# Hybrid trunk on one core: weight sums take the raw weights' place in the seven-product pairs, early parts get a room, 19 such pairs instead of 17

## The chip, the cores and the metric

The kernel runs on one core of one Trainium2 chip. The metric is the device time of one execution in microseconds (us); the median of three runs is the kernel's time.

## The reference

Two layers act on 256 tokens of 1024 channels: an attention layer and a convolution layer, each followed by an expert mixer ("peer"). What matters here is the mixer's last step. Every token has a gate for some of 16384 experts; the kernel computes all experts densely, so the last line below is, for each layer, one product of a gated activation matrix (256 tokens x 16384 experts) with `expert_v` (16384 x 1024).

```python
def chunk(args):
    xc, ec, gc = args
    u = expert_u[ec]
    act = jax.nn.gelu(jnp.einsum('cd,chkd->chk', xc, u))
    w = gc.astype(xc.dtype) * act
    return jnp.einsum('chk,chkd->cd', w, expert_v[ec])
```

## The kernel before

Each layer's mixer has a first stage, which makes the gated activations (`st`, kept in SBUF with experts on the partitions), and a second stage, which multiplies them with `expert_v` and is called the V stage here. The V stage runs over 64 pairs of weight rows; one row is 128 experts x 1024 channels, 512 KB, and is one load (`raw`, 4 buffers in rotation, issued in order by SP's queue).

Products are float32 in three terms. A float32 operand is split into a high part, rounded to the format that TensorE reads (`hi` for weights, `xh` for activations, cast by ACT), and the remainder (`lo`, `xo`, subtracted by DVE). `mm3` issues hi x hi, hi x lo and lo x hi: three TensorE products of 128x128 by 128x512.

- An **ordinary pair** (`s2`, through `weights`) has 2 rows x 4 quarters of the output (2 token halves by 2 channel halves) x 3 terms = 24 products. For it ACT casts two rows and one activation tile of 512, and DVE makes two `lo` and one `xo`.
- A **seven-product pair** (`s2_seven`; its pair numbers stand in `FAST`) multiplies the two rows as a 2 x 2 block product in Strassen's manner: seven products instead of eight, 21 with the three terms. Before them DVE forms sums of activations (s1 to s4, in place in `st`, 128 columns each) and of weights (t1 to t4, 512 columns each, in a tile of their own, `mix`), and the operands 11, (21, 22), (t1, t3) and (t2, t4) are split: four `hi`/`lo` pairs, all from the rotating room `whl` with three buffers of each. Four of the seven products go to PSUM tiles `q` that collect over all such pairs; `seven_end` adds them into the residual `x` after the last.

The activation parts `xh`/`xo` of ordinary pairs lie in two halves that alternate with the pair's number; a seven-product pair has a third part of its own. So ACT's cast for a pair must wait until TensorE's last product that reads the same part.

Which engine does what, and in which order, is written out at build time: each engine has one instruction stream, whose order a scheduler in the framework fixes; on the chip each stream is followed in order, with semaphore waits for operands and for buffers. In the second half of the first layer's V stage ACT also makes diagonal matrices for the next convolution (`diagonal`), three to a pair.

Of the kernel before, what the change touches and what calls it, by code (L numbers as in the profile page):

```python
# [7 lines left out]
F32 = mybir.dt.float32  # L8
F32R = mybir.dt.float32r
# [6 lines left out]
P = 128  # L16
D = 1024
# [25 lines left out]
G1 = 60  # L43
OH = 3 * NK * TB

FAST = (3, 6, 10, 13, 17, 20, 24, 27, 30, 34, 38, 41, 45, 48, 52, 55, 59)
TMP = 512 + NT * D


# [9 lines left out]
class Trunk:  # L59
# [32 lines left out]
        return cut  # L92


    def load(self, src):
        raw = self.wraw.tile([P, D], F32, tag="raw", name=self.nm("raw"))
        self.last_load = self.nc.sync.dma_start(raw, src)
        return raw

# [88 lines left out]
    def s2_seven(self, acc, q, srcs, a, at, parts, first, last):  # L188

        nc = self.nc
        sub = lambda o, x, y: nc.vector.tensor_tensor(o, x, y, op=ALU.subtract)  # L197
        s1, s2, s4, a11, a21, a12, a22 = (a[:, at + k * P:at + (k + 1) * P] for k in range(-3, 4))
        nc.vector.tensor_tensor(s1, a21, a22, op=ALU.add)
        sub(s2, s1, a11)  # L200
        sub(s4, a12, s2)
        sub(a21, a11, a21)
        ah, ao = parts
        seven = a[:, at - 3 * P:at + 4 * P]
        nc.scalar.copy(ah, seven)
        sub(ao, seven, ah.bitcast(F32))
        A = {k: (ah[:, n * P:(n + 1) * P], ao[:, n * P:(n + 1) * P])
             for n, k in enumerate(("s1", "s2", "s4", "11", "s3", "12", "22"))}
        left, right = slice(0, 512), slice(512, D)
        t1, t3, t2, t4 = (self.mix[:, k, :] for k in range(4))  # L210
        r1, r2 = (self.load(s) for s in srcs)
        sub(t1, r1[:, right], r1[:, left])
        sub(t3, r2[:, right], r1[:, right])
        sub(t2, r2[:, right], t1)
        sub(t4, r2[:, left], t2)
        B = {}
        for v, names in ((r1[:, left], ("11",)), (r2, ("21", "22")),
                         (self.mix[:, 0:2, :].rearrange("p k n -> p (k n)"), ("t1", "t3")),
                         (self.mix[:, 2:4, :].rearrange("p k n -> p (k n)"), ("t2", "t4"))):
            n = 512 * len(names)  # L220
            hi, lo = (self.whl.tile([P, D], F32R, tag=k, name=self.nm(k))[:, 0:n] for k in ("hi", "lo"))
            nc.scalar.copy(hi, v)  # L222
            sub(lo, v, hi.bitcast(F32))
            for k, name in enumerate(names):
                ks = slice(512 * k, 512 * k + 512)
                B[name] = hi[:, ks], lo[:, ks]
        for to, x, y in ((q[1], "11", "11"), (acc[0][0], "12", "21"), (acc[0][1], "s4", "22"),
                         (q[5], "s1", "t1"), (q[7], "s3", "t3"), (q[6], "s2", "t2"), (acc[1][0], "22", "t4")):
            mine = any(to is v for v in q.values())
            self.mm3(to, A[x], B[y], first and mine, last and mine)  # L230

    def seven_end(self, q):

        nc = self.nc
        x = lambda t, h: self.x[:, t, h * 512:(h + 1) * 512]
        one, u = self.mix[:, 0, :], self.mix[:, 1, :]
        add = lambda o, v, w: nc.vector.tensor_tensor(o, v, w, op=ALU.add)
        nc.scalar.copy(one, q[1])
        add(u, q[6], one)
        add(x(0, 0), x(0, 0), one)  # L240
        add(x(0, 1), x(0, 1), u)
        add(x(0, 1), q[5], x(0, 1))
        add(u, q[7], u)
        add(x(1, 0), x(1, 0), u)
        add(x(1, 1), x(1, 1), u)
        add(x(1, 1), q[5], x(1, 1))
# [383 lines left out]
    def peer(self, l, acc):  # L630
        nc, I = self.nc, self.I
        new = lambda: self.store_tile("st").rearrange("p (i t) -> p i t", t=T)
        st = [new()]
        sl = lambda i: st[i // HI][:, i % HI:i % HI + 2, :]

        g = self.gain(2 * l + 1, st[0][:, HI - D // T:, :].rearrange("p i t -> p (i t)"))
        xT = self.norm_T(g, acc)
        U, V = I["u"][l], I["v"][l]
        self.route_open(l)
        for h in range(PH):  # L640
            ps = self.s1_pair([I["wpq"][l, 2 * h], I["wpq"][l, 2 * h + 1]], xT, POOL_Q, h == 0)
            qT = self.qT[h % 2]
            nc.scalar.copy(qT, ps)
            self.route_scores(l, h, qT)
        route = self.route_steps()
        steps = 2 * (PH + 13)
        nb = T // TB
        half = NK // 4
        done = 0
        for pi in range(NK // 2):  # L650
            if pi == G0:
                for _ in route:
                    pass
                st.append(new())
                self.gates_open()
                self.one_hots(0)
            due = min(max(0, pi + 1 - G0) * nb // (G1 - G0), nb)
            todo = list(range(done, due))
            done = due
            ps = self.s1_pair([U[2 * pi], U[2 * pi + 1]], xT,  # L660
                              between=lambda j: [self.gate_bank(b, j, 2 * pi, st) for b in todo])
            for b in todo:
                if b + 1 < nb:
                    self.one_hots(b + 1)
            self.expert_rows(ps, sl(2 * pi), done * TB)
            if pi < G0:
                for _ in range((pi + 1) * steps // G0 - pi * steps // G0):
                    next(route, None)
        acc = self.s2_open()

        wh, wo = (self.one.tile([P, KC * T], F32R, tag=k, name=self.nm(k)) for k in ("xh", "xo"))
        w0 = self.work.tile([P, 2, 2 * T], F32R, tag="oh", name=self.nm("w0"))
        for pi in range(NK // 2):
            flat = st[2 * pi // HI].rearrange("p i t -> p (i t)")
            at = 2 * pi % HI * T
            if pi in FAST:
                fast = slice(4 * T, 4 * T + 7 * P)
                if pi == FAST[0]:
                    self.mix = self.work.tile([P, 4, 512], F32, tag="oh", name=self.nm("mix"))
                    quarters = {k: pool.tile([P, 512], F32, tag=tag, name=self.nm("q"))  # L680
                                for k, pool, tag in ((1, self.ps_m, "ps_m"), (5, self.ps_m, "ps_m"),
                                                     (7, self.ps_h, "ps_h"), (6, self.ps_h, "ps_h"))}
                self.s2_seven(acc, quarters, (V[2 * pi], V[2 * pi + 1]), flat, at, (wh[:, fast], wo[:, fast]),
                              pi == FAST[0], pi == FAST[-1])
            else:
                n = 2 * T
                r = pi % 2 * n

                h, o = (wh[:, r:r + n], wo[:, r:r + n]) if pi else (w0[:, 0], w0[:, 1])
                nc.scalar.copy(h, flat[:, at:at + n])  # L690
                nc.vector.tensor_tensor(o, flat[:, at:at + n], h.bitcast(F32), op=ALU.subtract)  # L691
                parts = [(h[:, j * T:(j + 1) * T], o[:, j * T:(j + 1) * T]) for j in range(2)]
                self.s2(acc, V, parts, 2 * pi, NK)
            if pi == FAST[-1] + 1:
                self.seven_end(quarters)
            if pi < half:
                pass
            elif l + 1 == DEPTH:
                if pi == half:
                    self.g_out = self.gain(2 * DEPTH, self.store_tile("g")[:, 0:D])  # L700
            else:
                if pi == half:
                    prep = self.conv_prep(l + 1)
                for _ in range(-(-(CDG + 1) // half)):
                    next(prep, None)
        return acc
# [280 lines left out]
```

## Time and profile before

| what | value |
|---|---|
| median of three runs | 1868.29 us (1867.66 to 1871.61) |
| profiled execution, its own time | 1868.77 us |
| span of that execution in the profile | 1866.8 us |
| mean granted TensorE clock | 0.996 |
| PE (TensorE products) busy | 1836.3 us, 98% |
| DVE (VectorE) busy | 1484.6 us, 80% |
| ACT (ScalarE) busy | 1006.1 us, 54% |

The span runs from the first to the last instruction; about 2 us of the execution's time lie outside it. PE's busy time counts products that overlap in the pipeline, so the distance between the starts of products, not their length, tells how fast TensorE goes. PEld is its weight load, which runs ahead of the product; an idle time before a PEld row is where TensorE's own queue waits.

### The profile page before, as it was taken

The numbers are of one execution on the slowest core, as the hardware profiler recorded it, in microseconds if no ns is written. First come the engines' busy times: TensorE is split into PE (matmuls) and PEld (weight loads), VectorE is DVE, ScalarE is ACT, GpSimd is POOL, SyncE is SP. The second block draws the span as 40 slices with busy tenths as digits, with TensorE's granted clock in tenths as the row PEclk, the third lists the DMA queues.
The fourth block names the chain that finished last, engine by engine and source line by source line (L and its number), as shares of the span: only waits on it lengthen the run. The fifth ranks groups of instructions, "written<-read, shape, count | busy, mean of one in ns | idle before, by whom it ended". The sixth has DMA issues, their size and how long they took to land. (4 is left out here: it accounts for less than half of the span.)

```text
span 1866.8 us, 32407 instructions
## 1 busy us (share of the span) xinstructions
PE 1836.3 (98%) x12566; PEld 1667.5 (89%) x12566; DVE 1484.6 (80%) x2857; ACT 1006.1 (54%) x1499; POOL 146.2 (8%) x107
## 2 busy tenths in 40 slices
PE   8999999999999999999999899999999999999998
PEld 6879999999999878877798799999999998888786
DVE  4669984788896888888887599847888968888887
ACT  4753455554445565777563534555544455655564
POOL 1213000000000000000076430000000000000000
PEclk9999999999999999999999999999999999999999
DMA  7445555444445656655542355554444456565654
GB/s 271 137 140 177 180 182 182 160 158 159 162 154 181 199 186 208 210 191 194 192 147 68 121 184 173 190 181 159 159 159 159 159 170 210 190 207 197 201 194 142
DMA packets 91738, 326.33 MB, mean 175 GB/s; under 512 B 10176, under 2 KB 12480, under 8 KB 91584
## 3 DMA queue, kind: packets, MB, share of 16 engines
q1 hardware_dynamic: 91584, 324.26, 51.6%
q8 instruction: 98, 1.61, 0.4%
q14 instruction: 56, 0.46, 0.1%
HBM read 323.17 MB, written 1.05 MB: 174 GB/s over the span
## 5 line engine op out<-in xcount | busy, mean ns | idle before, releaser
L108 ACT CAST hi<-raw 128x1024 fp32r<-128x1024 f32 x532 | 557.0, 1049 | 540.6 <-PE ps_h L148 409.3
L148 PE MATMUL ps_h<-xh,hi 128*128 128x256 f32 x2560 | 734.9, 288 | 0.0
L114 DVE TENSOR_TENSOR lo<-raw,hi 128x1024 fp32r<-128x1024 f32 x486 | 592.5, 1221 | 172.3 <-ACT hi L108 170.5
L148 PE MATMUL ps_h<-xh,lo 128*128 128x256 f32 x2560 | 721.5, 283 | 0.0
L148 PE MATMUL ps_h<-xo,hi 128*128 128x256 f32 x2560 | 718.1, 283 | 0.0
L148 PEld LDWEIGHTS ps_h<-xh,hi 128*128 128x128 f32 x2560 | 490.4, 192 | 2.0 <-issue 1.0
L148 PEld LDWEIGHTS ps_h<-xh,lo 128*128 128x128 f32 x2560 | 490.0, 192 | 0.0
L148 PEld LDWEIGHTS ps_h<-xo,hi 128*128 128x128 f32 x2560 | 488.0, 192 | 0.2
L133 PE MATMUL acc<-lo,xh 128*128 128x512 f32 x870 | 338.8, 391 | 1.2 <-DVE lo L197 1.1
L134 PE MATMUL acc<-hi,xo 128*128 128x512 f32 x870 | 337.9, 390 | 0.0
L132 PE MATMUL acc<-hi,xh 128*128 128x512 f32 x870 | 248.8, 391 | 0.0
L133 PEld LDWEIGHTS acc<-lo,xh 128*128 128x128 f32 x870 | 163.5, 188 | 38.2 <-DVE lo L197 2.7
L132 PEld LDWEIGHTS acc<-hi,xh 128*128 128x128 f32 x870 | 163.5, 188 | 34.3 <-ACT hi L108 0.5
L134 PEld LDWEIGHTS acc<-hi,xo 128*128 128x128 f32 x870 | 163.7, 188 | 33.8
L114 POOL TENSOR_TENSOR lo<-raw,hi 128x1024 fp32r<-128x1024 f32 x46 | 109.5, 2387 | 136.3 <-ACT hi L108 117.3
L690 ACT CAST xh<-st 128x512 fp32r<-128x512 f32 x92 | 57.2, 623 | 115.0 <-PE acc L133 115.0
L290 POOL TENSOR_TENSOR sums<-sums,mhalf 128x1 f32<-128x1 f32 x10 | 8.7, 871 | 989.9 <-DVE sums L287 989.9
L691 DVE TENSOR_TENSOR xo<-st,xh 128x512 fp32r<-128x512 f32 x92 | 63.1, 688 | 27.6 <-ACT xh L690 27.5
L197 DVE TENSOR_TENSOR lo<-mix,hi 128x1024 fp32r<-128x1024 f32 x68 | 80.2, 1221 | 5.4 <-ACT hi L222 5.4
L857 DVE TENSOR_TENSOR oh<-iota,slot 128x1024 f16<-128x1024 f16 x64 | 44.3, 692 | 47.8 <-PE ps_g L869 47.8
L869 PE MATMUL ps_g<-oh 128*128 128x128 f16 x1024 | 81.5, 220 | 0.0
L877 DVE SCALAR_TENSOR_TENSOR st<-ps_g,st 128x256 f32<-128x256 f32 (+4 forms) x224 | 74.5, 351 | 8.5 <-PE ps_g L869 8.4
(183 smaller groups left out, 1857.5 us busy)
## 6 DMA issues: line engine op xcount, KB each, us to landing
raw<-in_u_dram SPq DMA_DIRECT2D x256, 512.0 KB, 3.2
raw<-in_v_dram SPq DMA_DIRECT2D x256, 512.0 KB, 4.2
raw<-in_wpq_dram SPq DMA_DIRECT2D x32, 512.0 KB, 3.5
raw<-in_pw_dram SPq DMA_DIRECT2D x24, 512.0 KB, 3.4
raw<-in_wqk_dram SPq DMA_DIRECT2D x16, 512.0 KB, 3.5
raw<-in_wv_dram SPq DMA_DIRECT2D x8, 512.0 KB, 6.6
raw<-in_wo_dram SPq DMA_DIRECT2D x8, 512.0 KB, 3.2
att<-in_bias_dram SPq DMA_DIRECT2D x4, 512.0 KB, 9.1
```

The lines of the kernel that those rows point to most:

```text
L108: ins = [nc.scalar.copy(hi, raw)]
L114: ins.append(eng.tensor_tensor(lo, raw, hi.bitcast(F32), op=ALU.subtract))
L132: return [mm(ps, wh, xh, start=first, stop=False), mm(ps, wh, xo, start=False, stop=False), mm(ps, wo, xh, start=False, stop=last)]
L133: mm(ps, wh, xo, start=False, stop=False),
L134: mm(ps, wo, xh, start=False, stop=last)]
L148: self.nc.tensor.matmul(ps[:, j, :], w[:, c * P:(c + 1) * P], x[:, c, :], start=n == 0, stop=n == len(terms) - 1)
L197: sub = lambda o, x, y: nc.vector.tensor_tensor(o, x, y, op=ALU.subtract)
L690: nc.scalar.copy(h, flat[:, at:at + n])
L691: nc.vector.tensor_tensor(o, flat[:, at:at + n], h.bitcast(F32), op=ALU.subtract)
L857: nc.vector.tensor_tensor(g0, iota, slot(0), op=ALU.is_equal)
L869: nc.tensor.matmul(ps[:, t, :], self.oh[:, b % 2, 0, tp, :, e], self.oh[:, b % 2, 1 + k, tp, :, e], start=k == 0, stop=k == 1)
L877: nc.vector.scalar_tensor_tensor(v, ps[:, :, lo:lo + m].rearrange("p t i -> p i t"), 1.0 / GS, v, op0=ALU.mult, op1=ALU.mult)
```

## The change

`FAST` becomes every third pair, 3 to 57, 19 in each layer instead of 17. In `s2_seven` the sums t1 and t3 overwrite the first raw row and t2 and t4 the second, so `mix` goes; `split` casts and subtracts as before. The parts of the first three weight operands (11, t1 and t3) lie in a tile of their own, `early_room`, which takes the place that `mix` had in SBUF; only (21, 22) and (t4, t2) still take buffers of `whl`. The products stand in another order: the three of `early_room` first. `seven_end` takes its scratch from the `raw` buffers.

```diff
-FAST = (3, 6, 10, 13, 17, 20, 24, 27, 30, 34, 38, 41, 45, 48, 52, 55, 59)
+FAST = tuple(range(3, 60, 3))
...
-        t1, t3, t2, t4 = (self.mix[:, k, :] for k in range(4))
         r1, r2 = (self.load(s) for s in srcs)
-        sub(t1, r1[:, right], r1[:, left])
-        sub(t3, r2[:, right], r1[:, right])
-        sub(t2, r2[:, right], t1)
-        sub(t4, r2[:, left], t2)
-        B = {}
-        for v, names in ((r1[:, left], ("11",)), (r2, ("21", "22")),
-                         (self.mix[:, 0:2, :].rearrange("p k n -> p (k n)"), ("t1", "t3")),
-                         (self.mix[:, 2:4, :].rearrange("p k n -> p (k n)"), ("t2", "t4"))):
-            n = 512 * len(names)
-            hi, lo = (self.whl.tile([P, D], F32R, tag=k, name=self.nm(k))[:, 0:n] for k in ("hi", "lo"))
+
+        def split(v, room, *names):
+            hi, lo = room
             nc.scalar.copy(hi, v)
             sub(lo, v, hi.bitcast(F32))
             for k, name in enumerate(names):
                 ks = slice(512 * k, 512 * k + 512)
                 B[name] = hi[:, ks], lo[:, ks]
-        for to, x, y in ((q[1], "11", "11"), (acc[0][0], "12", "21"), (acc[0][1], "s4", "22"),
-                         (q[5], "s1", "t1"), (q[7], "s3", "t3"), (q[6], "s2", "t2"), (acc[1][0], "22", "t4")):
+        B = {}
+        slot = lambda: [self.whl.tile([P, D], F32R, tag=k, name=self.nm(k)) for k in ("hi", "lo")]
+        split(r1[:, left], self.early_room[0], "11")
+        sub(r1[:, left], r1[:, right], r1[:, left])
+        sub(r1[:, right], r2[:, right], r1[:, right])
+        split(r1, self.early_room[1], "t1", "t3")
+        split(r2, slot(), "21", "22")
+        sub(r2[:, right], r2[:, right], r1[:, left])
+        sub(r2[:, left], r2[:, left], r2[:, right])
+        split(r2, slot(), "t4", "t2")
+        for to, x, y in ((q[1], "11", "11"), (q[5], "s1", "t1"), (q[7], "s3", "t3"), (acc[0][0], "12", "21"),
+                         (acc[0][1], "s4", "22"), (q[6], "s2", "t2"), (acc[1][0], "22", "t4")):
...
-        one, u = self.mix[:, 0, :], self.mix[:, 1, :]
+        room = self.load_room()
+        one, u = room[:, 0:512], room[:, 512:D]
...
-                    self.mix = self.work.tile([P, 4, 512], F32, tag="oh", name=self.nm("mix"))
+                    cut = self.cutter(self.work.tile([P, 6 * 512], F32R, tag="oh", name=self.nm("early")))
+                    self.early_room = [(cut(n), cut(n)) for n in (512, D)]
```

DVE's stream at pair 45 of the second layer, before. The names raw_18732 and raw_18734 are the pair's own two rows; raw_18690 and raw_18696 are the rows of the ordinary pair ahead of it.

```order
L691 TENSOR_TENSOR xo_16851<-st_13397,xh_16850 128x512
L197 TENSOR_TENSOR mix_16967<-raw_18732 128x512
L199 TENSOR_TENSOR st_13397<-st_13397 128x128
L114 TENSOR_TENSOR lo_18693<-raw_18690,hi_18692 128x1024
L197 TENSOR_TENSOR st_13397<-st_13397 128x128 x2
L197 TENSOR_TENSOR mix_16967<-raw_18734,raw_18732 128x512
L197 TENSOR_TENSOR mix_16967<-raw_18734,mix_16967 128x512
L197 TENSOR_TENSOR st_13397<-st_13397 128x128
L114 TENSOR_TENSOR lo_18699<-raw_18696,hi_18698 128x1024
L197 TENSOR_TENSOR mix_16967<-raw_18734,mix_16967 128x512
```

The same place now; raw_18653 and raw_18655 are the pair's rows, raw_18617 is the second row of the pair ahead.

```order
L117 TENSOR_TENSOR lo_18620<-raw_18617,hi_18619 128x1024
L200 TENSOR_TENSOR early_16918<-raw_18653,early_16918 128x512
L200 TENSOR_TENSOR raw_18653<-raw_18653 128x512
L701 TENSOR_TENSOR xo_16802<-st_13348,xh_16801 128x512
L200 TENSOR_TENSOR raw_18653<-raw_18655,raw_18653 128x512
L200 TENSOR_TENSOR lo_18664<-raw_18655,hi_18663 128x1024
L202 TENSOR_TENSOR st_13348<-st_13348 128x128
L200 TENSOR_TENSOR early_16918<-raw_18653,early_16918 128x1024
L200 TENSOR_TENSOR raw_18655<-raw_18655,raw_18653 128x512
L200 TENSOR_TENSOR st_13348<-st_13348 128x128 x2
L200 TENSOR_TENSOR raw_18655<-raw_18655 128x512
L200 TENSOR_TENSOR st_13348<-st_13348 128x128
```

The first sum of weights stood ahead of both `lo` of the ordinary pair; now every instruction on the seven-product pair's rows stands behind them, and the rows are used in the order in which they are loaded. Behind the second list follow one `xo` of an ordinary pair and the `lo` of (t4, t2).

PE's stream at the same pair, before: hi_18748 is (t1, t3), hi_18752 is (t2, t4), hi_18781 the next pair's first row.

```order
L132 MATMUL q_16969<-hi_18748,xh_16850 128x512
L132 MATMUL q_16970<-hi_18748,xh_16850 128x512
L132 MATMUL q_16971<-hi_18752,xh_16850 128x512
L132 MATMUL acc_16848<-hi_18752,xh_16850 128x512
L133 MATMUL q_16969<-lo_18749,xh_16850 128x512
L134 MATMUL q_16969<-hi_18748,xo_16851 128x512
```

And now: the early tile is (t1, t3), hi_18663 is (21, 22), hi_18669 is (t4, t2), hi_18698 the next pair's first row.

```order
L135 MATMUL q_16920<-early_16918,xh_16801 128x512
L135 MATMUL q_16921<-early_16918,xh_16801 128x512
L136 MATMUL acc_16797<-lo_18664,xh_16801 128x512
L137 MATMUL acc_16797<-hi_18663,xo_16802 128x512
L136 MATMUL acc_16798<-lo_18664,xh_16801 128x512
L137 MATMUL acc_16798<-hi_18663,xo_16802 128x512
L136 MATMUL q_16920<-early_16918,xh_16801 128x512
L137 MATMUL q_16920<-early_16918,xo_16802 128x512
L136 MATMUL q_16921<-early_16918,xh_16801 128x512
L137 MATMUL q_16921<-early_16918,xo_16802 128x512
L135 MATMUL q_16922<-hi_18669,xh_16801 128x512
L135 MATMUL acc_16799<-hi_18669,xh_16801 128x512
```

Between the first product that needs the high part of (t1, t3) and the first that needs that of the last operand stood one product; now nine stand there.

## Rows read from the trace of the kernel before

**Rows 1.** The page's busy times and granted clock in 40 slices.

```profile
PE 1836.3 (98%) x12566; PEld 1667.5 (89%) x12566; DVE 1484.6 (80%) x2857; ACT 1006.1 (54%) x1499; POOL 146.2 (8%) x107
PEclk9999999999999999999999999999999999999999
```

**Rows 2.** Timeline: the first and the last product of both V stages (start, length).

```profile
586.62 0.40 PE L132 MATMUL acc<-hi,w 128*128 128x512 f32 x1
...
929.98 0.39 PE L134 MATMUL acc<-hi,xo 128*128 128x512 f32 x1
...
1517.68 0.40 PE L132 MATMUL acc<-hi,w 128*128 128x512 f32 x1
...
1859.02 0.39 PE L134 MATMUL acc<-hi,xo 128*128 128x512 f32 x1
```

**Rows 3.** Chain that ended last: two rows' first products, 12 products apart.

```profile
1557.70 0.91 PE acc L132 x4
1560.42 0.91 PE acc L132 x4
```

**Rows 4.** Windows, second layer: from one seven-product pair to the next.

```profile
1536.23:1552.07 15.84, 15.84 (x71) 12.88 (x70) 13.62 (x16) 9.69 (x12) 0.00 (x0) 1.00 0.54 181
1552.07:1573.34 21.27, 21.27 (x94) 17.38 (x94) 17.92 (x27) 12.41 (x15) 0.00 (x0) 1.00 0.59 195
1573.34:1589.22 15.88, 15.88 (x70) 12.79 (x70) 13.88 (x16) 9.68 (x12) 0.00 (x0) 1.00 0.71 216
```

**Rows 5.** Timeline of the seven-product pair at 1552.

```profile
1549.84 0.62 ACT L690 CAST xh<-st 128x512 fp32r<-128x512 f32 x1 [1.44 <-PE acc L133]
1550.36 2.00 ACT L222 CAST hi<-mix 128x1024 fp32r<-128x1024 f32 x2
1551.90 1.01 PE L132 MATMUL q<-hi,xh 128*128 128x512 f32 x3
1552.41 0.19 PEld L132 LDWEIGHTS q<-hi,xh 128*128 128x128 f32 x1 [0.32 <-ACT hi L222]
```

**Rows 6.** Waits of the weight load: total us, times, longest.

```profile
PEld q L132 <- ACT hi L222: 9.5, 30, 0.3
PEld q L133 <- DVE lo L197: 6.1, 17, 0.7
```

**Rows 7.** DVE's timeline ahead of pair 45 of the second layer.

```profile
1746.87 0.69 DVE L691 TENSOR_TENSOR xo<-st,xh 128x512 fp32r<-128x512 f32 x1 [0.84 <-ACT xh L690]
1749.77 0.69 DVE L197 TENSOR_TENSOR mix<-raw 128x512 f32<-128x512 f32 x1 [2.20 <-DMA raw<-in_v_dram]
1750.38 0.29 DVE L199 TENSOR_TENSOR st<-st 128x128 f32<-128x128 f32 x1
1750.58 1.22 DVE L114 TENSOR_TENSOR lo<-raw,hi 128x1024 fp32r<-128x1024 f32 x1
```

**Rows 8.** The chain behind it: the load, and TensorE at its end.

```profile
1744.02 5.72 DMA raw<-in_v_dram
...
1761.29 0.50 PE q L133
```

**Rows 9.** Groups by form, 1540 to 1840: DVE, then ACT.

```profile
L114 DVE TENSOR_TENSOR lo<-raw,hi 128x1024 fp32r<-128x1024 f32 x81 | 99.0, 1222 | 12.8 <-ACT hi L108 12.2
L691 DVE TENSOR_TENSOR xo<-st,xh 128x512 fp32r<-128x512 f32 x40 | 27.5, 688 | 12.5 <-ACT xh L690 12.4
L197 DVE TENSOR_TENSOR xo<-st,xh 128x896 fp32r<-128x896 f32 x16 | 17.4, 1088 | 0.3
L197 DVE TENSOR_TENSOR st<-st 128x128 f32<-128x128 f32 x45 | 11.1, 285 | 0.0
L108 ACT CAST hi<-raw 128x1024 fp32r<-128x1024 f32 x81 | 85.2, 1052 | 40.4 <-PE acc L134 27.2 <-PE q L134 13.2
L690 ACT CAST xh<-st 128x512 fp32r<-128x512 f32 x40 | 25.0, 624 | 56.8 <-PE acc L133 56.8
```

**Rows 10.** The V rows' loads, from issue to landing, both layers.

```profile
DMA to landing us min/median/max: 3.0/4.2/6.0
```

**Rows 11.** ACT's timeline, first layer: diagonals between casts.

```profile
791.92 0.99 ACT L485 ACTIVATE conv<-ident,conv 128x128 f32<-128x128 f32 x3
792.82 2.06 ACT L108 CAST hi<-raw 128x1024 fp32r<-128x1024 f32 x2
```

More of the change, by code (lines that the diff above doesn't have):

```diff
@@ L92, in cutter, with load_room @@
         return cut
+    def load_room(self):
+        return self.wraw.tile([P, D], F32, tag="raw", name=self.nm("raw"))
     def load(self, src):
-        raw = self.wraw.tile([P, D], F32, tag="raw", name=self.nm("raw"))
+        raw = self.load_room()
         self.last_load = self.nc.sync.dma_start(raw, src)
```

## The prediction

> **What bounds the kernel now.** I read the page first: TensorE is busy 98% of the span at full granted clock in every slice, DVE 80%, ACT 54% [rows 1]. So time can be won only by giving TensorE fewer products or by closing gaps between them. The edit touches only the V stages, and the order of the streams outside them is the same, so the rest of the 1866.8 us stays.
>
> The timeline gives the size of the V stages. From first start to last start plus one spacing they take 343.6 and 341.6 us [rows 2]. The chain gives the spacing: twelve products lie 2.72 us apart, 0.2267 us each [rows 3]. By the code a stage has 47 x 24 + 17 x 21 = 1485 products, so 336.6 us without a gap. The gaps are therefore 7.0 + 5.0 = 12.0 us in both stages together, and the question is which of them the edit closes or opens.
>
> Windows from one seven-product pair to the next show the regular part. A cycle of three pairs has 21 + 48 = 69 products, 15.64 us, and took 15.84 and 15.88; one of four has 93, 21.08, and took 21.27 [rows 4]. That is some 0.2 us for each seven-product pair, 34 x 0.2 = 6.8 of the 12.0 us. Its place is in rows 5: TensorE's weight load waits 0.32 us for ACT's second cast of `mix`. ACT had stood 1.44 us waiting for TensorE before casting an activation part, and both 1 us casts of weight sums are queued behind that; TensorE wants them one product apart [rows 5]. The waits count 30 such cases [rows 6].
>
> The other 5.2 us are single stops. The longest in the second layer shows how they arise: DVE's stream has the sum for pair 45 ahead of the `lo` of the ordinary pair before it; DVE stood 2.20 us until that sum's raw row was there, and the `lo` behind it came late too [rows 7]. The load had taken 5.72 us, and 11.5 us after that sum's start TensorE stopped at a `q` product [rows 8].
>
> **The change, part by part.** *Two more seven-product pairs in each layer.* Each replaces 24 products by 21: 4 x 3 x 0.2267 = **2.7 us** less on TensorE, certain as long as TensorE is the bound. The stages then hold 2 x 1479 products, 670.5 us without a gap, against 685.2 now.
>
> *DVE's load.* A cycle is now always one seven-product and two ordinary pairs. DVE does in it seven subtractions of 1024 (1.22 us), seven of 512 (0.69), one of 896 (1.09) and four of 128 (0.285): 15.6 us by length [rows 9], nearly all of TensorE's 15.64. But behind a 0.69 us instruction the next starts 0.61 later, and behind a 0.285 us one 0.20 later [rows 7], so 19 x 0.08 = 1.5 comes off: 14.1 us. The three-pair cycles of before had DVE busy 13.6 and 13.9 us [rows 4], the same. Sums of weights in place cost what they cost in `mix`: same size, same engine. DVE so has 1.5 us to spare in a cycle, where a four-pair cycle has more (17.92 of 21.27): the relief that every second cycle had is gone.
>
> The Trainium skill's page "VectorE: DVE Perf Modes", section "The DRAIN you can't avoid", says the next VectorE instruction does not start until the pipe of the one before has emptied. By that the 15.6 us would stand and DVE would be full; the starts in the trace contradict it by 0.08 us an instruction.
>
> *The order of the products and the early room.* I laid one steady cycle out by hand from the orders and rows 9. TensorE starts the second ordinary pair at 0 and leaves it at 5.67 (24 products and one of the next). Then come (11), the high parts of (21, 22) and (t1, t3), eight products with low parts, and the high part of (t4, t2) is wanted at 8.84, its low part at 9.97. ACT may cast the activations that reuse the pair's part at 5.67, is done at 6.29, casts (t4, t2) by 7.35 (1.05), and DVE's `lo` is done at 8.6 with the semaphore's way. So both stand ready 1.4 us early, where ACT was 0.3 late before. The operand (t1, t3) no longer waits for a buffer of `whl` and is cast before that stop. The regular gap should vanish: **-6.8 us**.
>
> It comes back in part in the first layer's second half. There three diagonals (0.90 us from start to start) stand between the cast of (t4, t2) and that of the next pair's first row [rows 11]; that row would be ready at 9.4 and is wanted at 9.29. With the semaphore I put 0.25 us on each of the ten pairs from 30 to 57: **+2.5**. Bounds: 0, if a stop elsewhere gives ACT time, to 0.9 us each, the whole row of diagonals, 9 us.
>
> *The raw buffers.* The second raw row is now held until the `lo` of (t4, t2), at 8.6 in my cycle, instead of (21, 22); the load that reuses it lands 4.2 us later, at 12.8, at worst 6.0 [rows 10], at 14.6. ACT can use it only at 12.9, when a `hi` buffer is freed, so a median load costs nothing. The worst makes DVE 1.7 late. About 0.5 is taken up where DVE waits for the cast of (t4, t2), and 1.4 is the margin there: just covered. Against that, no sum stands ahead of an ordinary `lo` any more, so a late load no longer delays work on rows that have landed. Of the 5.2 us of single stops I take half as gone, **-2.6**, between 0 (loads come later) and 5.2.
>
> *The rest* I cost at nothing. `early_room` waits for the same buffer as `mix` did (pair 0's parts). `seven_end` has the same additions, but takes one of four raw buffers; the cover is three rows of finished weights ahead of TensorE, about 2.7 us each. Without it one load of 4.2 us would show, in each layer.
>
> **Sum.** -2.7 - 6.8 + 2.5 - 2.6 = -9.6. From the profiled execution's 1868.8 that gives 1859.2, and as it lay 0.5 above the median, 1858.7; I say **1859**.
>
> **The rivals.** *Nothing but the products* (1865.6): the gaps change place. For it: the held raw row, and the fact that ACT's stops for TensorE remain. Against it: the 1.4 us of margin. Below 1864.6 or above 1872.0 (0.2%) a measurement of this kernel can tell a time from no change; this lies inside.
>
> *DVE becomes the bound* (slower). Before, DVE was idle 2.0 to 2.2 us in a three-pair cycle [rows 4], and a four-pair cycle followed. If that idle time cannot shrink, because DVE stands for casts and raw rows in the chain 11, t1, t3, t2, t4, a cycle takes 14.1 + 2.1 = 16.2. With 18 cycles a layer that is 36 x 0.56 = 20 us over the 670.5, 690.7 instead of 685.2: 1874. It decides at a cycle of 16.05 us (14.7 / 36 = 0.41 over 15.64). For it: 90% load with a serial chain. Against it: the idle time of before is largely DVE waiting for ACT that waits for TensorE [rows 9], which follows TensorE when that gets faster.
>
> *Every gap closes*: diagonals and loads hide too. 670.5 and 1 us at the ends is 13.7 less: 1855.
>
> **Chances and range.** Forecast, 1856 to 1863: 0.53. Every gap closes: 0.13. Between forecast and no change (1863 to 1864.6): 0.10. Only the products, or gaps anew: 0.14. DVE bound: 0.10. Faster 0.76, within 0.2% 0.14, slower 0.10. The range, 1854.5 to 1867, leaves out the slower case and little beside it.
>
> **What would show it.** Windows from one seven-product pair to the next of 15.65 to 15.75 us in the second layer, some 0.2 to 0.3 more in the first's second half; no 0.3 us waits at the q product of the last operand; DVE at 13.6 to 14.2 us in each. Wrong would be: cycles of 16 us or more with PE waiting for a `lo` (DVE bound), loads near 6 us with DVE waiting for raw rows, or a new wait at the next pair's first row in the second layer.

## The result and the profile after

The changed kernel took 1857.88 us (median of five runs, 1857.14 to 1859.85) against 1869.95 us of the kernel before in the same rounds. The ratio is 0.9942 with a 95% interval of 0.9931 to 0.9953, so it is 0.5 to 0.7% faster. The profiled execution spans 1855.5 us, 11.3 less than before.

The page's busy times after; the granted clock stands at 9 in every slice, as in [rows 1], which means 90% or more (1.00 in the windows below):

```profile
PE 1825.4 (98%) x12554; PEld 1668.0 (90%) x12554; DVE 1506.0 (81%) x2897; ACT 1015.0 (55%) x1507; POOL 146.3 (8%) x107
```

TensorE's share is the same 98%: the page alone would not show where the time went. The windows do: first both V stages, then two cycles of the second layer. The columns are the window, its length, the busy time of PE, PEld, DVE, ACT and POOL, the granted clock, the DMA share and GB/s.

```profile
587.10:924.92 337.82, 336.73 (x1481) 276.91 (x1479) 300.69 (x394) 224.34 (x306) 0.60 (x3) 1.00 0.61 202
1511.68:1847.87 336.19, 336.14 (x1481) 277.04 (x1479) 299.92 (x393) 204.82 (x234) 0.27 (x1) 1.00 0.58 194
1541.85:1557.49 15.64, 15.64 (x70) 12.95 (x69) 14.31 (x20) 9.80 (x11) 0.00 (x0) 1.00 0.63 201
1557.49:1573.13 15.64, 15.64 (x70) 12.95 (x69) 14.29 (x19) 9.85 (x11) 0.00 (x0) 1.00 0.59 202
```

The V stages went from 343.6 + 341.6 to 337.8 + 336.2 us, 11.2 us less, which is the whole gain. With 2958 products at 0.2267 us, 670.5, the gaps are 3.5 us where they were 12.0. A cycle of three pairs takes 15.64 us, exactly its 69 products, where [rows 4] had 15.84 and 15.88; DVE is busy 14.3 us of it.

The weight load's waits at the `q` products (total us, cases, longest), first for DVE's `lo`, then for ACT's cast. They stood in [rows 6] with 17 and 30 cases:

```profile
PEld q L136 <- DVE lo L200: 1.5, 2, 1.0
PEld q L135 <- ACT hi L217: 1.1, 2, 0.7
```

The timeline of one seven-product pair in the second layer answers to [rows 5]. It shows ACT's cast of an activation part, of (t4, t2), DVE's `lo` of it, and the product that needs the high part:

```profile
1637.95 0.62 ACT L700 CAST xh<-st 128x512 fp32r<-128x512 f32 x1 [2.22 <-PE acc L136]
1638.80 1.05 ACT L217 CAST hi<-raw 128x1024 fp32r<-128x1024 f32 x1 [0.23 <-DVE raw L200]
1639.89 1.23 DVE L200 TENSOR_TENSOR lo<-raw,hi 128x1024 fp32r<-128x1024 f32 x1 [0.37 <-ACT hi L217]
1641.15 0.39 PE L135 MATMUL q<-hi,xh 128*128 128x512 f32 x1
```

ACT still stops for TensorE before the activation part, even longer than before, but one cast is left behind that stop instead of two. It ends at 1639.85, 1.3 us before TensorE wants it.

### The profile page after: what moved, and what is told of

Its sections match the earlier page's. It is cut to its first block, busy times and chain, and to the rows that moved or that the text cites. A ratio compares the mean times of both kernels' runs of the same rounds, so it can differ in the third digit from the quotient of the medians.

```text
span 1855.5 us, 32473 instructions
## 1 busy us (share of the span) xinstructions
PE 1825.4 (98%) x12554; PEld 1668.0 (90%) x12554; DVE 1506.0 (81%) x2897; ACT 1015.0 (55%) x1507; POOL 146.3 (8%) x107
## 5 line engine op out<-in xcount | busy, mean ns | idle before, releaser
L111 ACT CAST hi<-raw 128x1024 fp32r<-128x1024 f32 x524 | 544.7, 1048 | 496.1 <-PE ps_h L151 409.4
L117 DVE TENSOR_TENSOR lo<-raw,hi 128x1024 fp32r<-128x1024 f32 x478 | 579.8, 1221 | 165.5 <-ACT hi L111 161.1
L136 PE MATMUL acc<-lo,xh 128*128 128x512 f32 x850 | 330.5, 390 | 0.1
L137 PE MATMUL acc<-hi,xo 128*128 128x512 f32 x850 | 330.0, 390 | 0.0
L135 PE MATMUL acc<-hi,xh 128*128 128x512 f32 x850 | 240.7, 391 | 0.3 <-ACT hi L111 0.2
L135 PEld LDWEIGHTS acc<-hi,xh 128*128 128x128 f32 x850 | 159.3, 188 | 35.9 <-ACT hi L111 2.6
L137 PEld LDWEIGHTS acc<-hi,xo 128*128 128x128 f32 x850 | 159.9, 188 | 33.2
L200 DVE TENSOR_TENSOR lo<-raw,hi 128x1024 fp32r<-128x1024 f32 x76 | 92.8, 1221 | 10.8 <-ACT hi L217 10.7
L217 ACT CAST early<-raw 128x512 fp32r<-128x512 f32 x76 | 63.6, 837 | 60.1 <-DVE raw L200 39.5
L217 ACT CAST hi<-raw 128x1024 fp32r<-128x1024 f32 x76 | 79.9, 1052 | 23.3 <-DVE raw L200 17.3
```

Source lines behind the costliest of these rows:

```text
L111: ins = [nc.scalar.copy(hi, raw)]
L117: ins.append(eng.tensor_tensor(lo, raw, hi.bitcast(F32), op=ALU.subtract))
L135: return [mm(ps, wh, xh, start=first, stop=False), mm(ps, wh, xo, start=False, stop=False), mm(ps, wo, xh, start=False, stop=last)]
L136: mm(ps, wh, xo, start=False, stop=False),
L137: mm(ps, wo, xh, start=False, stop=last)]
```

## The experiments

V stages are both together, from the first start to the last start plus 0.2267 us; gaps are what exceeds the products.

| run | what it is | V stages, us | gaps, us | time, us | ratio to before (95%) |
|---|---|---|---|---|---|
| before | | 685.2 | 12.0 | 1869.95 | |
| after | | 674.0 | 3.5 | 1857.88 | 0.9942 (0.9931 to 0.9953) |
| e1_old_code_19 | old code, new spacing | 679.8 | 9.3 | 1864.81 | 0.9969 (0.9958 to 0.9979) |
| e2_new_code_17 | new code, old spacing | 677.1 | 3.9 | 1862.34 | 0.9958 (0.9944 to 0.9971) |
| e3_no_early_room | new code without the room | 806.8 | 136 | 1990.98 | 1.0638 (1.0620 to 1.0657) |
| e4_old_product_order | same streams as after | 672.7 | 2.3 | 1859.46 | 0.9943 (0.9930 to 0.9957) |
| e5_dve_plus_1us | DVE +1.0 us a cycle | 677.4 | 7.0 | 1863.74 | 0.9960 (0.9944 to 0.9976) |
| e6_dve_plus_2us | DVE +2.0 us a cycle | 733.5 | 63 | 1919.34 | 1.0257 (1.0240 to 1.0273) |
| e7_22_pairs | 22 pairs | 703.1 | 37 | 1888.73 | 1.0099 (1.0082 to 1.0115) |
| e8_20_pairs | 20 pairs | 674.0 | 4.9 | 1858.30 | 0.9931 (0.9917 to 0.9945) |
| e9_old_stream_order | room, old order on TensorE | 676.8 | 6.3 | 1862.25 | 0.9956 (0.9942 to 0.9969) |

My theory: the regular gap goes because of how the operands are handled, the products give 2.7 us, and DVE has about 1.5 us a cycle to spare. The rivals: the number or spacing of the pairs does it; the room alone or the order alone does it; DVE is at its limit.

**Each half of the change alone.** The first run is the old code with the new spacing, the second the new code with the old one:

```diff
-FAST = (3, 6, 10, 13, 17, 20, 24, 27, 30, 34, 38, 41, 45, 48, 52, 55, 59)
+FAST = tuple(range(3, 60, 3))
```

> The code of before (tile mix, four operands from whl, old order of products) with the new FAST, 19 seven-product pairs at every third pair. If the gain came from the new operand handling, only 2.7 us of products go and the regular gap of 0.2 us stays at all 38 pairs, with the single stops at least as long as before: V stages of 683 to 688 us together (685.2 before, 674.0 after), time 1866 to 1871 us. If the larger number of such pairs were the main thing, it would stand near after: below 1861 us.

> The code of after with the old FAST of 17 pairs. By my steps 2 x 1485 products, 673.2 us without a gap, and the 3.5 us of gaps that after still has, or fewer, since every second cycle has four pairs: 675 to 677 us of V stages, 1859 to 1861 us, 2 to 3 us slower than after. If the even spacing of the pairs removed the gaps, they would return here: 1864 us or more.

A window of the old code with the new spacing, then its weight load's wait for ACT's cast (total us, cases, longest):

```profile
1564.18:1580.01 15.83, 15.83 (x70) 12.87 (x69) 14.20 (x19) 9.68 (x12) 0.00 (x0) 1.00 0.66 200
```

```profile
PEld q L132 <- ACT hi L222: 11.4, 37, 0.3
```

Two windows of the new code with the old spacing:

```profile
1603.69:1619.33 15.64, 15.64 (x70) 12.95 (x69) 14.61 (x21) 9.85 (x12) 0.00 (x0) 1.00 0.60 201
1619.33:1640.41 21.08, 21.08 (x94) 17.46 (x93) 17.39 (x22) 12.44 (x14) 0.00 (x0) 1.00 0.60 201
```

The old code keeps its 0.19 us at every pair, 37 waits for 38 pairs: the regular gap belongs to the code and not to the spacing. The new code has none at 15.64 and 21.08 us; its V stages and its time lie just above what I expected. But the old code did better than expected, 679.8 instead of 683 to 688: 9.3 - 38 x 0.19 leaves 2.1 us of single stops where before had 5.2. So the new spacing alone also takes away single stops. With the old spacing, the pair's first sum of weights stood ahead of two ordinary `lo` on DVE only behind three ordinary pairs, as at pair 45, and ahead of one behind two; with the even spacing it stands ahead of one everywhere but at each layer's first pair. I did not separate that order from the spacing.

**Without the early room.** The operands 11 and (t1, t3) go back to the rotating buffers, the sums stay in place:

```diff
-        split(r1[:, left], self.early_room[0], "11")
+        split(r1[:, left], [v[:, 0:512] for v in slot()], "11")
...
-        split(r1, self.early_room[1], "t1", "t3")
+        split(r1, slot(), "t1", "t3")
```

> The code of after, but 11 and (t1, t3) take buffers of whl as before, so a cycle takes eight instead of six of its rotating three; the order of the products is the new one in the code. If the room carries the gain: the next pair's first row takes the buffer of (t1, t3), which is read late in the new order, so a gap of 0.5 to 1 us opens at each of the 38 pairs: V stages 690 to 710 us, 1873 to 1893 us, slower than before. If only the order and the sums in place matter, it stands within 2 us of after.

It is far slower than I expected, and by another wait. First two windows, one cycle each (the granted clock is the third number from the end), then the weight load's largest wait, then from the timeline TensorE's first product of the pair, ACT's casts of (21, 22) and of (t4, t2), and the product that needs the last:

```profile
1636.66:1656.59 19.93, 18.11 (x70) 13.85 (x69) 14.70 (x20) 9.64 (x12) 0.00 (x0) 0.91 0.49 159
1656.59:1674.92 18.33, 16.50 (x70) 12.71 (x69) 14.71 (x20) 9.67 (x12) 0.00 (x0) 1.00 0.52 172
```

```profile
PEld q L135 <- ACT hi L217: 69.9, 38, 1.9
```

```profile
1636.66 0.39 PE L135 MATMUL q<-hi,xh 128*128 128x512 f32 x1
1637.16 1.04 ACT L217 CAST hi<-raw 128x1024 fp32r<-128x1024 f32 x1
...
1641.02 1.04 ACT L217 CAST hi<-raw 128x1024 fp32r<-128x1024 f32 x1 [2.82 <-DVE raw L200]
...
1642.12 0.51 PE L135 MATMUL q<-hi,xh 128*128 128x512 f32 x1 [1.41 <-ACT hi L217]
```

The cast of (21, 22) and TensorE's first product of a pair in the changed kernel:

```profile
1633.31 1.05 ACT L217 CAST hi<-raw 128x1024 fp32r<-128x1024 f32 x1 [0.40 <-DMA raw<-in_v_dram]
...
1635.93 0.39 PE L135 MATMUL q<-early,xh 128*128 128x512 f32 x1
```

The gap is not at the next pair's first row but at (t4, t2), in every pair. Sums in place can start only when the raw values have been cast and subtracted, and that now waits for a buffer. By the rotation of three, (21, 22) takes the buffer of the ordinary pair's second row, which TensorE reads to the end of that pair: its cast starts 0.50 us behind TensorE's first product of the pair, where the changed kernel has it 2.62 us ahead. (The activation cast ahead of it on ACT waits for TensorE at the same point.) Then follow the subtraction, two sums, the cast and the product, one after the other. ACT stands 2.82 us for the sums and TensorE 1.41 us for ACT. With `mix` and no room (old code, same spacing) a cycle takes 15.83 us. So the sums in place are bearable only together with the room. The other half, a room beside `mix`, was not run.

**The order of the products.** In the code the order (11, 21, 22, t1, t3, t2, t4) was put back:

```diff
-        for to, x, y in ((q[1], "11", "11"), (q[5], "s1", "t1"), (q[7], "s3", "t3"), (acc[0][0], "12", "21"),
-                         (acc[0][1], "s4", "22"), (q[6], "s2", "t2"), (acc[1][0], "22", "t4")):
+        for to, x, y in ((q[1], "11", "11"), (acc[0][0], "12", "21"), (acc[0][1], "s4", "22"),
+                         (q[5], "s1", "t1"), (q[7], "s3", "t3"), (q[6], "s2", "t2"), (acc[1][0], "22", "t4")):
```

> The code of after with the products in the old order (11, 21, 22, t1, t3, t2, t4), the early room kept. By the hand-laid cycle (t4, t2) is then wanted some 0.5 us earlier, at about 8.4 against 7.4 when it is ready, so the room alone still closes the regular gap: V stages 674 to 676 us, within 2 us of after. If it is the order of the products that takes the casts out of each other's way, the gap of 0.2 us returns at 38 pairs: 681 us, 1864 to 1866 us.

This tells nothing of the order: the scheduler makes the same five streams of it, row for row, as of the changed kernel. It is a second measurement of that kernel, and useful as such: 672.7 against 674.0 us, so 1.3 us between two traces of the same streams mean nothing.

The order was then forced, with issue-order dependencies between the products:

```diff
...
+        for to, x, y in four:
+            high = mm(to, A[x][0], B[y][0], start=first and mine(to), stop=False)
+            self.after(high, prev)
+            prev = high
+        for to, x, y in four:
+            self.after(mm(to, A[x][0], B[y][1], start=False, stop=False), prev)
+            self.after(mm(to, A[x][1], B[y][0], start=False, stop=last and mine(to)), prev)
```

> The code of after, early room and sums in place, but TensorE's stream forced to stand as before at the seven-product pairs: all products of (21, 22) first, then the four high products of (t1, t3) and (t4, t2) one behind the other, then their low ones. (The order of the products in the code of e4 did not reach the chip: the scheduler laid all five streams exactly as in after.) The high part of (t4, t2) is then wanted at about 7.9 in my cycle instead of 8.84, and was ready at 7.4 to 7.8. If the room alone closes the regular gap, cycles stay at 15.64 to 15.7 and the V stages at 673 to 677 us, within 3 us of after. If the nine products between are what covers the cast, cycles of 15.8 to 15.9 come back: 680 to 684 us, 1864 to 1868 us.

Two windows, then the weight load's waits, then from the timeline the stop in the second window (ACT's cast of (21, 22), of (t4, t2), and the weight load):

```profile
1623.14:1638.78 15.64, 15.64 (x70) 12.95 (x69) 14.42 (x21) 9.89 (x11) 0.00 (x0) 1.00 0.60 203
1748.86:1765.43 16.57, 15.94 (x71) 12.88 (x69) 15.03 (x20) 10.12 (x12) 0.00 (x0) 1.00 0.57 189
```

```profile
PEld q L242 <- ACT hi L217: 7.4, 14, 1.6
```

```profile
1747.52 1.05 ACT L217 CAST hi<-raw 128x1024 fp32r<-128x1024 f32 x1 [1.69 <-DMA raw<-in_v_dram]
...
1752.86 1.05 ACT L217 CAST hi<-raw 128x1024 fp32r<-128x1024 f32 x1 [1.37 <-DVE raw L200]
...
1753.96 0.19 PEld L242 LDWEIGHTS q<-hi,xh 128*128 128x128 f32 x1 [1.06 <-ACT hi L217]
```

The regular gap does not come back: with the room and the sums in place, most cycles stay within 0.1 us of 15.64 in either order. What the order gives is margin. TensorE wants (t4, t2) about 0.9 us earlier here, and a load that is 1.69 us late now reaches it: 14 waits where after has 2, and gaps of 6.3 us against 3.5 and 2.3.

**How near DVE is to its limit.** The 896-column subtraction of each seven-product pair is done two or three times, with the same result:

```diff
         sub(ao, seven, ah.bitcast(F32))
+        sub(ao, seven, ah.bitcast(F32))
```

> The code of after, with the 896-column subtraction of each seven-product pair done twice (same result): 1.0 us more for DVE in each cycle of three pairs, nothing else. In the trace of after a cycle is 15.64 us with DVE busy 13.4 to 14.7. If DVE has some 1 us to spare, this is nearly hidden: cycles of 15.64 to 15.8, V stages 674 to 680 us, 1858 to 1864 us. If DVE's chain already sets the cycle, 1 us shows in each of 38: about 1896 us.

> The same subtraction done three times: 2.0 us more for DVE in each cycle, 16.3 to 16.7 us of work against 15.64 of products. DVE becomes the bound: cycles of 16.4 to 17, 36 x 0.8 to 1.4 = 28 to 50 us more than after, 1886 to 1908 us. If DVE had as much to spare as the 80% on the page would suggest, it would still stand near 1858.

A window of each, first with 1.0 us more and then with 2.0:

```profile
1547.73:1563.37 15.64, 15.64 (x70) 12.95 (x69) 15.17 (x22) 9.88 (x11) 0.00 (x0) 1.00 0.59 201
```

```profile
1580.91:1597.67 16.76, 15.94 (x70) 12.87 (x69) 16.18 (x22) 9.74 (x11) 0.00 (x0) 1.00 0.56 186
```

One more microsecond is hidden, but for 3.4 us over both stages; the second costs 56 us more, beyond what I expected. All of the 3.4 us lies where ACT also makes diagonals. The stretch from pair 33 to pair 57 of the first layer, 552 products, first with 1.0 us more and then in the changed kernel:

```profile
759.99:890.24 130.25, 128.21 (x553) 102.60 (x552) 123.46 (x162) 96.88 (x158) 0.00 (x0) 1.00 0.60 197
```

```profile
759.12:885.71 126.59, 125.98 (x554) 103.26 (x552) 115.78 (x154) 97.60 (x158) 0.00 (x0) 1.00 0.61 200
```

Outside that stretch the limit lies between 1 and 2 us a cycle above what the change asks of DVE. In both runs the scheduler also laid DVE's stream in another order, so neither step is DVE's load alone.

**More pairs.** First 22 pairs with steps of 3, 3 and 2, then a twentieth, pair 60:

```diff
-FAST = tuple(range(3, 60, 3))
+FAST = (3, 6, 9, 11, 14, 17, 19, 22, 25, 27, 30, 33, 35, 38, 41, 43, 46, 49, 51, 54, 57, 59)
```

> The code of after with 22 seven-product pairs, steps of 3, 3 and 2 in turn and 59 as the last: 18 products fewer, 4.1 us. A step of two has 45 products, 10.2 us, for about 11.1 of DVE; eight pairs have 41.5 us of products for some 39 to 40 of DVE. If DVE catches up in the steps of three, 1854 to 1857 us. If it can't, 0.9 us or more shows at each of the 14 steps of two: 1866 us or more.

> The code of after with pair 60 as a twentieth: 6 products fewer, 1.4 us, so 1856 to 1857 us if the end can take it. The eight additions into x (5.5 us of DVE) then fall into the last three pairs; if DVE is late there, up to 2 us of each stage's end come back and it is no faster than after.

With 22 pairs, a step of two with the step of three behind it, the step of two by itself, the other step of three, and the first stop of the pair behind the step of two:

```profile
1575.03:1603.18 28.15, 26.70 (x115) 21.16 (x114) 25.39 (x35) 16.64 (x19) 0.00 (x0) 1.00 0.55 187
1575.03:1585.23 10.20, 10.20 (x47) 8.45 (x45) 10.13 (x19) 6.09 (x7) 0.00 (x0) 1.00 0.49 159
1603.18:1618.82 15.64, 15.64 (x70) 12.95 (x69) 14.68 (x21) 10.02 (x12) 0.00 (x0) 1.00 0.61 201
```

```profile
1590.38 0.19 PEld L136 LDWEIGHTS q<-early,xh 128*128 128x128 f32 x1 [1.11 <-DVE early L200]
```

The two steps have 45 + 69 = 114 products, 25.84 us, and take 28.15. DVE's 25.39 us of work would fit in both. The short step itself takes its 10.20 us, with DVE busy 10.13 of them; the stops come in the pair behind it, where DVE is late, and they aren't won back. The price is 2.3 us for 0.68 gained. The twentieth pair is no faster than after by this measurement: its trace has 1.4 us fewer products and 1.4 us more gaps. No version here is clearly faster than the changed kernel.

## Why the prediction was right

The forecast was 1859, the time 1857.9. That the two lie so near is in part luck. The kernel before measured 1.7 us more in these rounds than the 1868.29 I had started from, and the gain was 11.3 us by the spans and 12.1 by the medians, where my terms add up to 9.6: one gave 2.5 us too little and another 0.9 too much. Term by term:

- **2.7 us of products**: as worked out. The new code with 17 pairs stands 3 to 4 us above the two traces with 19, gaps included.
- **The regular gap, 6.8 us**: gone, and for the reason given: one of ACT's two casts no longer stands behind its stop for TensorE. I had put it on the order and the room together. The forced order shows that the new order is not needed for it: the room with the sums in place is enough. The order keeps the margin, 1.3 us in the rows above against the 1.4 of my hand-laid cycle.
- **2.5 us back in the first layer's second half**: mis-sized, no pair there has a regular gap. I had taken the second layer's TensorE stream for both. A cycle there, then ACT's diagonals and next casts there, and TensorE's first product with (t4, t2) and with the next pair's first row:

```profile
840.22:855.86 15.64, 15.64 (x70) 12.95 (x69) 13.39 (x18) 11.73 (x20) 0.00 (x0) 1.00 0.62 203
```

```profile
841.67 0.98 ACT L494 ACTIVATE conv<-ident,conv 128x128 f32<-128x128 f32 x3
842.56 1.99 ACT L111 CAST hi<-raw 128x1024 fp32r<-128x1024 f32 x2
...
842.72 0.39 PE L135 MATMUL q<-hi,xh 128*128 128x512 f32 x1
...
844.98 1.07 PE L135 MATMUL acc<-hi,xh 128*128 128x512 f32 x4
```

The next row is wanted 2.26 us behind (t4, t2), not 0.45: the scheduler has put the low products ahead of it. ACT has that row at about 843.6, 1.4 us early. With 1.0 us more work for DVE this half did lose time, as shown above.

- **Single stops, 2.6 of 5.2**: 1.7 in this trace (3.5 us left), 2.9 in the second trace of the same streams. The 3.5 us are a few stops. The two largest, about 1.1 us each, are in the first layer, and both stand behind late loads, the cause that I named. At the first: ACT's cast of operand 11, of (t4, t2), and the weight load behind it. At the second, pair 33: the weight load's waits for both parts of (t4, t2).

```profile
614.37 0.62 ACT L217 CAST early<-raw 128x512 fp32r<-128x512 f32 x1 [2.19 <-DMA raw<-in_v_dram]
...
621.82 1.05 ACT L217 CAST hi<-raw 128x1024 fp32r<-128x1024 f32 x1 [1.91 <-DVE raw L200]
622.92 0.19 PEld L135 LDWEIGHTS q<-hi,xh 128*128 128x128 f32 x1 [0.69 <-ACT hi L217]
...
764.45 0.19 PEld L135 LDWEIGHTS q<-hi,xh 128*128 128x128 f32 x1 [0.39 <-ACT hi L217]
765.71 0.19 PEld L136 LDWEIGHTS q<-lo,xh 128*128 128x128 f32 x1 [0.96 <-DVE lo L200]
```

The two rows of each of these pairs, from issue to landing, and then all V rows, which took a little longer than in [rows 10]:

```profile
DMA to landing us min/median/max: 6.2/6.3/6.4
DMA to landing us min/median/max: 5.6/5.7/5.8
```

```profile
DMA to landing us min/median/max: 3.0/4.4/6.4
```

The stop at pair 33 is no chance of one trace: it comes back there with the order forced, with 20 pairs and in the second trace of the same streams. Just ahead of its rows SP's queue issues two loads for the next convolution (747.5 and 747.9); no run moved them, so their part is not shown. The even spacing, which the old code shows to remove single stops too, I had not counted as a cause. The two halves seem to overlap: 5.4 and 8.1 us alone, 11.2 together, or 12.5 in the second trace. That is 1.0 to 2.3 us, and two traces of the same streams differ by 1.3.

- **DVE**: 14.1 us expected in a cycle, 14.3 measured in the second layer's windows and 13.4 in the first layer's. What I called 1.5 us to spare is between 1 and 2 by the added work. The rival that DVE becomes the bound was as far away: its threshold was set at a cycle of 16.05 us, and the run with 2.0 us more reached 16.76. In the Trainium skill's page "VectorE: DVE Perf Modes", the section "The DRAIN you can't avoid", which I cited against my sum, also says that a next instruction that is not held starts earlier. So the 0.08 us of overlap in the trace need not contradict it.

## What to carry to other kernels

Where a nearly full engine shows the same small gap at every repetition, look at what the engine that feeds it has queued behind its own stop; a place of its own for the operands that can be made early moves their casts ahead of that stop. Margin against late loads is a second thing, which here the order on the consumer gave. Read the order in the built streams and not in the code, and in each stretch apart: one experiment here changed the code and no stream, and one term failed because two layers had different streams.

## What the runs showed that I had not expected

Without the early room TensorE's granted clock fell in some cycles, 0.91 in the window above and 0.978 over that run, where before has 0.996. Behind that run's 1.41 us wait, products for a while start 0.43 us apart instead of 0.23:

```profile
1644.66 0.63 PE L136 MATMUL acc<-lo,xh 128*128 128x512 f32 x1
1645.09 0.63 PE L137 MATMUL acc<-hi,xo 128*128 128x512 f32 x1
```

That is the lower of the two levels, 1.2 GHz. In the trace of after the V stages have 1.00 throughout. So part of that run's loss lies in a clock that fell after a stop, and not in the stops alone: of the two cycles shown above, the one at 0.91 took 19.93 us and the one at 1.00 18.33. The stop by itself does not settle it, for in the next cycle a wait of the same length was followed by products 0.23 us apart:

```profile
1662.06 0.49 PE L135 MATMUL q<-hi,xh 128*128 128x512 f32 x1 [1.41 <-ACT hi L217]
...
1664.04 0.39 PE L137 MATMUL q<-hi,xo 128*128 128x512 f32 x1
1664.27 0.39 PE L136 MATMUL acc<-lo,xh 128*128 128x512 f32 x1
```
